# Two transformer blocks in one program: when clears, dense tables, gathers and a branch are placed

## The chip, the cores and the metric

The kernel runs on one core of a Trainium2 chip. The metric is the time of one execution on the device, in microseconds; the number before the change is the median of three runs. One more execution was recorded by the hardware profiler. Its trace gives each instruction's start and duration on the core's engines: PE (TensorE, matrix products and transposes), DVE (VectorE), ACT (ScalarE), POOL (GpSimd) and SP (SyncE, which here only issues DMAs). ACT and POOL issue DMAs too, each in its own instruction stream, in order.

## The reference

The input x has 512 tokens of 1024 channels, everything in fp32. Cut to what matters here:

```
first block:   h = rms_norm(x);  u = h @ w_in
               x += [rms(conv(u)), rms(attention(u))] @ w_out      # 12 heads of 64
               x += cross_attention(rms(x), rms(mem))              # 256 memory tokens
               x += moe(rms(x), w1, w3, w2)                        # 32 experts, 1024 x 512
               x  = rms_norm(x) * final_norm_g
second block:  z = rms(x) @ w_in_2                                 # q, k, v, f, u_ssm, two gates
               x += (sig(g1) * forgetting_attention @ w_a
                     + sig(g2) * s5(u_ssm) @ w_s) @ w_out_2
               x += moe(rms(x), w_gate, w_up, w_down)              # 32 experts, 1024 x 256
moe:           per token: best of 4 groups, then 2 of its 8 experts;
               y[token] += gate * (silu(x w1) * (x w3)) w2
```

## The kernel before, in words

**Stages.** `dense1` computes the first block up to its experts, `m1.run` the experts, `dense2` the second block up to its experts, `m2.run` those; at the end SP stores X in four DMAs. The residual X stays on chip as 4 tiles of 128 tokens x 1024. A planner that simulates a timeline orders each engine's instructions from the order of the program; `tc.issue_after(i)` adds, to what is traced in the block on the engine of instruction `i`, an order behind `i`. It gives no order to instructions of another engine.

**Dense products** are made in three passes (L114 to L116) of a high and a low part of the operands (`mm3`). Weights come in units of 1 MB by SP into a ring of two buffers (L141); ACT casts the high part (`wh`, L125), DVE or POOL subtracts the low part (`wl`, L128).

**Start.** `dense1` loads x, two weight units and the memory tokens, transposes x (L227), casts it to columns (ACT L202, DVE L203), sums its squares (ACT L236), and computes masks and rotary tables on DVE. Then come six rounds, each with two heads (`attend`): scores, a maximum on DVE (L541), an exponential on ACT (L542) for each of four row blocks, transposes, a copy by ACT (L550), the product with v; weight units of later rounds are traced between.

**Experts** (`Moe`). The 32 experts go in 16 pairs; a pair's 128 rows are 64 slots of either expert. Before the experts the rows of X and, behind them, the routing weights are written to DRAM (`rows`, 1024 + 33 numbers a token). For a pair, `slots` computes on DVE for each slot its token (or none), `fetch` gathers the rows by an indirect DMA on POOL's queue (L1161), `columns` transposes them, `up` and `down` are the matmuls (L1083, L1105). A slot with no token gathers row 0. The result of a pair is either written to a table `y` in DRAM (`made` in the trace) by an indirect DMA with a bound that drops empty slots (`store`, L1136), or added to X by one-hot matmuls (`scatter`, L1120 to L1123); pairs 14 and 15 are scattered. `y` is cleared beforehand by 16 DMAs of 512 KB on ACT's queue (`clear`, L805). Near the end SP reads `y` back (`load_made`, L1064), in its list of weight loads ahead of the last 4 (first block) or 2 (second block) loads, and DVE adds it to X (`add_made`, L1070). `rest` is a branch with a loop for tokens beyond an expert's 64 slots; the second block computes one such unit always (at pair 9) and enters the loop only for more. Then the last pair is finished (`finish`).

**Second block's start.** Three tables for the state space part are computed during the first experts and written to DRAM: WT and Qs (2 MB each, read back by `ssm.fetch` on ACT's queue, L1403) and M (2 MB, read in 8 DMAs on POOL's queue by `load_M`, L1713). They live in `big_r`, a pool of two 2 MB buffers that the experts' weights use before. WT feeds `states` (L1653), M and Qs feed `outputs` (L1690, L1691). Meanwhile X is transposed and cast (L1758, L202), `norms` computes two norms by a chain of tiny DVE operations (`rsq`, L212 to L219), and X is scaled by ACT (L1846) and POOL (L1847).

**Names in the trace.** `k.last` is the last scatter cast on ACT (L1115). `marks` and `exps` hold the score matmuls and the exponentials. `wfh` (L1747) is a small cast on POOL at the second block's start.

Of the kernel before, what the change touches and what calls it, by code (L numbers as in the profile page):

```python
# [10 lines left out]
F32 = mybir.dt.float32  # L11
# [11 lines left out]
S = 512  # L23
NB = 4
# [343 lines left out]
def dense1(k, a, Xt, m1, m2, ring1, more, dram, dbg):  # L368
# [15 lines left out]
    with ExitStack() as st:  # L384
# [72 lines left out]
        with ExitStack() as s0:  # L457
# [61 lines left out]

            marks = []  # L520

# [5 lines left out]
            def attend(g, h, om, mid=iter(())):  # L527
# [5 lines left out]
                for b in range(NB):  # L533
# [7 lines left out]
                    V.tensor_tensor_reduce(ml, p, lnm[:, lo:lo + 512], -0.125, 3.0e38, op0=OP.add, op1=OP.min, accum_out=nm)  # L541
                    nc.scalar.activation(ml, ml, AF.Exp, bias=nm, scale=-1.0, accum_out=den[:, b:b + 1])  # L542
                    pt = tpt()
# [72 lines left out]
            for g in range(6):  # L616
                om = wk.tile([128, NB, 128], F32, name="om", bufs=1)
                attend(g, 0, om)
                if m1 and g < 4:
                    with tc.issue_after(marks[-4]):  # L620
                        for m in (m1, m2):
                            for i in range(2):
                                m.clear(zero, 2 * g + i)
# [140 lines left out]
class Moe:  # L764
# [9 lines left out]
    spot = after_loads = None  # L774
    deep = 3

    def __init__(self, k, X, ff, w_a, w_b, w_down, gname, gain, wg, bg, wr, br, spare, rows, y):
# [256 lines left out]
    def ahead(self, wt, n, order=()):  # L1034

        self.wt, self.left = wt, n
        self.early = [self.places(2) for _ in range(16)]
        loads = [x for p, W in enumerate(self.early) for x in self.loads((2 * p, 2 * p + 1), W, wt, first=p == 0)]

        i = len(loads) - self.ff // 128  # L1040
        self.made = []
        loads[i:i] = [partial(self.load_made, b) for b in range(NB)]
        order = list(order)
        self.todo = [loads[i] for i in order] + loads[len(order):]
# [94 lines left out]
    def slots(self, wk, ps, n):  # L1139
# [8 lines left out]
        V.tensor_tensor(q[:, 2:3], ab[:, 0:1], ab[:, 1:2], op=OP.add)  # L1148
        V.tensor_scalar(q[:, 0:1], q[:, 2:3], -1.0, 0.0, op0=OP.add, op1=OP.max)
        V.tensor_scalar(q[:, 1:2], ab[:, 1:2], 0.0, float(S), op0=OP.is_gt, op1=OP.mult)  # L1150
        V.scalar_tensor_tensor(q[:, 1:2], q[:, 2:3], -1.0, q[:, 1:2], op0=OP.add, op1=OP.add)
        V.tensor_scalar(q[:, 3:4], q[:, 2:3], 0.0, k.i16[:, 8:9], op0=OP.is_equal, op1=OP.mult)
        V.tensor_add(q[:, 1:2], q[:, 1:2], q[:, 3:4])
        ids = wk.tile([128, 2], I32, name="ids", bufs=5)
        V.tensor_copy(ids, q[:, 0:2])
        return ids

    def fetch(self, pool, idx, name="xr", deep=3):

        xr = pool.tile([128, D + 33], F32, name=name, bufs=deep)  # L1160
        self.k.nc.gpsimd.indirect_dma_start(out=xr, out_offset=None, in_=self.rows, in_offset=bass.IndirectOffsetOnAxis(ap=idx, axis=0))  # L1161
        return xr
# [41 lines left out]
    def experts(self, wk, ps, between=None):  # L1204
# [7 lines left out]
        def fetch(n):  # L1212
            ids = self.slots(wk, ps, n)
            got[n] = (ids, self.fetch(wk, ids[:, 0:1], deep=deep) if n else None)

        for p in range(16):
# [22 lines left out]
            if last:  # L1239
                self.finish(wk, ps, *last)  # L1240
            last = (hg, W, parts, gate, got[p][0], self.slots_T(wk, p) if p >= 14 else None)
            if between:
# [5 lines left out]
            if self.spare and p == 9:  # L1248
                unit = self.extra_up(wk, ps, unit, self.wt, nc.sync)
                self.finish(wk, ps, *last)  # L1250
                last = unit
        self.add_made()
        if self.spare:
            self.rest(wk, ps, self.wt, self.wl)
        else:
            spare = self.room()
            self.rest(wk, ps, Slots([spare] * 2), spare)
        self.finish(wk, ps, *last)

# [125 lines left out]
class Ssm:  # L1385
# [12 lines left out]

    def fetch(self, big):

        t = [big.tile([128, KC, S], F32, name="b") for i in range(2)]
        for d, s in zip(t, self.par):
            self.k.nc.scalar.dma_start(d, s.rearrange("u p n -> p u n"))  # L1403
        self.WT, self.Qs = [x.rearrange("p u (t q n) -> p u t q n", t=2, q=2) for x in t]

# [310 lines left out]
def dense2(k, a, X, ssm, m2, early, dbg):  # L1716
# [4 lines left out]
    with ExitStack() as st:  # L1721
# [24 lines left out]
        wfh, wfl = w1.tile([128, KC, 8], F32R, name="wfh"), w1.tile([128, KC, 8], F32R, name="wfl")  # L1746
        G.tensor_copy(wfh, wf)  # L1747
        G.tensor_sub(wfl, wf, f(wfh))
# [71 lines left out]
        u_unit(0, ws)  # L1820
        ssm.fetch(k.big_r)

# [20 lines left out]
        with tc.issue_after(puts[-1].ins):  # L1843
            ssm.tables(w1)
        for b in range(NB):
            nc.scalar.activation(X[:, b], X[:, b], AF.Copy, scale=r1[:, b:b + 1])  # L1846
            G.tensor_tensor(X[:, b], X[:, b], frow, op=OP.mult)  # L1847
        gate_unit(sgs, 3080, 0)
# [20 lines left out]
        ssm.states(w1, sct, 1)  # L1869
        ssm.load_M(k.big_r)  # L1870
        gate_unit(sgs, 3080, 2)
# [3 lines left out]
        ssm.outputs(w1, sct, tpt, 1)  # L1875
        v_unit(1)

        ysT = k.big_r.tile([128, KC, S], F32R, name="b")
# [171 lines left out]
def whole(ctx, tc, a, out):  # L2050
# [8 lines left out]
             rows=dram.tile([S, D + 33], F32, name="xrow1"), y=dram.tile([2 * S + 128, D], F32, name="made1"))  # L2059
    m1.deep = 2  # L2060
    m2 = Moe(k, X, 256, a["w_expert_gate_2"][0], a["w_expert_up_2"][0], a["w_expert_down_2"][0], "norm_ffn_g_2",
             a["norm_ffn_g_2"][0], a["w_router_group_2"][0], a["b_router_group_2"][0], a["w_router_expert_2"][0], a["b_router_expert_2"][0], spare=True,
# [83 lines left out]
```

## Time and profile before

| | |
|---|---|
| median of 3 runs | 1786.28 us (1783.35 to 1787.2) |
| profiled execution, its own time | 1789.1 us |
| its span, first to last instruction | 1787.5 us |
| PE busy | 1578.6 us (88%) |
| DVE busy | 779.1 us (44%) |
| ACT busy | 548.0 us (31%) |
| POOL busy | 383.6 us (21%) |
| moved by DMA | 431.88 MB, 242 GB/s on average |
| mean granted TensorE clock | 0.963 of full |

The busy shares are averages over stages with different limits. By the windows, the stages are: the start to about 60 us; attention and cross attention to about 500 us; the first experts to about 1037 us; the second block's dense part to about 1490 us; its experts to the end. A row of waits says which instruction's end came last before an engine went on; "issue" there means that nothing in the profile explains the wait.

### The profile page before, as it was taken

To read this page: it belongs to the slowest core of one execution; us is meant where nothing else is said; L and a number is where in the kernel's file an instruction comes from. 1 tells how busy PE (TensorE), PEld (TensorE's weight loads), DVE (VectorE), ACT (ScalarE), POOL (GpSimd) and SP (SyncE) were. 2 spreads that over 40 slices of the span, in tenths; PEclk is the share of its full clock that TensorE was granted. 3 is DMA by queue.
4 is the path that set the end of the run, shared out by engine and by line. 5 is a ranking of instruction groups with operands and counts; after the bars stand their busy time and mean duration, and the time that the engine had idled before them with its cause. 6 is when DMAs were issued, how large, how long until landed. Compare 5 with 4: busy or idle time off the path is not lost. (4 is left out here: it accounts for less than half of the span.)

```text
span 1787.5 us, 24321 instructions
## 1 busy us (share of the span) xinstructions
PE 1578.6 (88%) x9257; PEld 1070.1 (60%) x9257; DVE 779.1 (44%) x1984; ACT 548.0 (31%) x1212; POOL 383.6 (21%) x523
## 2 busy tenths in 40 slices
PE   3899999999989998888888777899998998988986
PEld 2799999998983333233232245788997894333332
DVE  2896456655454511121110466714665537311225
ACT  2436656644321211010100042233556422111111
POOL 1131112011122631433240022201212401211110
PEclk8999999999999999999999998899999999998998
DMA  9323123232758999999999964625540846999994
GB/s 297 113 72 107 48 71 119 91 101 82 284 180 340 422 424 425 424 425 425 424 423 427 422 149 53 88 72 95 72 71 25 324 136 221 380 418 418 418 410 166
DMA packets 171080, 431.88 MB, mean 242 GB/s; under 512 B 18526, under 2 KB 105749, under 8 KB 143184
## 3 DMA queue, kind: packets, MB, share of 16 engines
q1 hardware_dynamic: 133616, 378.08, 58.0%
q0 software_dynamic: 11936, 32.21, 5.6%
q10 hardware_dynamic: 25408, 20.00, 3.5%
q8 instruction: 74, 1.21, 0.3%
q14 instruction: 46, 0.38, 0.1%
HBM read 403.38 MB, written 34.74 MB: 245 GB/s over the span
## 5 line engine op out<-in xcount | busy, mean ns | idle before, releaser
L1083 PE MATMUL h<-b,xgr 128*64 128x512 f32 x800 | 222.5, 600 | 23.4 <-DMA b<-in_w_dram 21.5
L115 PE MATMUL mm<-wl,b 128*128 128x256 f32 x832 | 236.5, 285 | 6.9 <-POOL wl L128 4.0
L1083 PE MATMUL h<-w,xgr 128*64 128x512 f32 (+1 forms) x752 | 221.4, 609 | 19.2 <-DMA w<-in_w_dram 14.1
L114 PE MATMUL mm<-wh,b 128*128 128x256 f32 x832 | 236.1, 286 | 2.4 <-DVE sgs L1803 0.9
L116 PE MATMUL mm<-wh,b 128*128 128x256 f32 x832 | 234.6, 284 | 0.0
L128 POOL TENSOR_TENSOR wl<-w,wh 128x1024 fp32r<-128x1024 f32 x38 | 97.1, 2556 | 516.2 <-ACT wh L125 445.2
L125 ACT ACTIVATE wh<-w 128x1024 fp32r<-128x1024 f32 x112 | 118.3, 1058 | 159.4 <-PE mm L115 67.6
L115 PEld LDWEIGHTS mm<-wl,b 128*128 128x128 f32 x832 | 159.0, 191 | 9.0 <-POOL wl L128 4.4
L114 PEld LDWEIGHTS mm<-wh,b 128*128 128x128 f32 x832 | 158.3, 191 | 4.6 <-DVE sgs L1803 1.1
L116 PEld LDWEIGHTS mm<-wh,b 128*128 128x128 f32 x832 | 158.4, 191 | 0.5
L114 PE MATMUL mm<-b,wh 128*128 128x512 f32 x320 | 127.4, 408 | 28.7 <-ACT b L202 15.9
L1105 PE MATMUL o<-b,hgT 128*64 128x512 f32 x448 | 129.9, 641 | 24.7 <-issue 8.9
L1083 PEld LDWEIGHTS h<-b,xgr 128*64 128x64 f32 x800 | 67.0, 137 | 134.1 <-issue 82.6
L1083 PEld LDWEIGHTS h<-w,xgr 128*64 128x64 f32 (+1 forms) x752 | 64.8, 140 | 130.8 <-issue 89.3
L1087 DVE SCALAR_TENSOR_TENSOR hg<-h,gate,hg 128x512 f32<-128x512 f32 (+1 forms) x32 | 19.7, 616 | 261.6 <-PE h L1083 196.6
L115 PE MATMUL mm<-b,wh 128*128 128x512 f32 x320 | 128.6, 403 | 0.0
L116 PE MATMUL mm<-b,wl 128*128 128x512 f32 x320 | 127.0, 402 | 0.2 <-POOL wl L128 0.2
L128 DVE TENSOR_TENSOR wl<-w,wh 128x1024 fp32r<-128x1024 f32 x74 | 94.4, 1276 | 52.8 <-ACT wh L125 52.3
L1105 PE MATMUL o<-w,hgT 128*64 128x512 f32 (+1 forms) x328 | 97.4, 622 | 5.3 <-ACT hgT L1099 2.1
L1105 PEld LDWEIGHTS o<-b,hgT 128*64 128x64 f32 x448 | 40.1, 146 | 87.4 <-issue 74.6
L114 PEld LDWEIGHTS mm<-b,wh 128*128 128x128 f32 x320 | 60.8, 192 | 44.8 <-ACT b L202 17.7
L1086 ACT ACTIVATE hg<-h,gate 128x512 f32<-128x512 f32 (+1 forms) x32 | 18.6, 580 | 220.1 <-PE h L1083 171.4
(673 smaller groups left out, 2791.6 us busy)
## 6 DMA issues: line engine op xcount, KB each, us to landing
b<-in_w_dram SPq DMA_DIRECT2D x106, 1024.0 KB
w<-in_w_dram SPq DMA_DIRECT2D x86, 1024.0 KB
b<-in_w_expert_down_dram SPq DMA_DIRECT2D x20, 1024.0 KB
w<-in_w_expert_gate_dram SPq DMA_DIRECT2D x36, 512.0 KB
w<-in_w_expert_up_dram SPq DMA_DIRECT2D x36, 512.0 KB
w<-in_w_in_dram SPq DMA_DIRECT2D x17, 1024.0 KB
b<-in_w_expert_gate_dram SPq DMA_DIRECT2D x30, 512.0 KB
b<-in_w_expert_up_dram SPq DMA_DIRECT2D x30, 512.0 KB
```

The lines of the kernel that those rows point to most:

```text
L114: nc.tensor.matmul(out, sh, mh, start=start, stop=False, skip_group_check=True)
L115: nc.tensor.matmul(out, sh, ml, start=False, stop=False, skip_group_check=True)
L116: nc.tensor.matmul(out, sl, mh, start=False, stop=stop, skip_group_check=True)
L125: nc.scalar.activation(hi[:, :kc, :n], src, AF.Copy)
L128: e.tensor_sub(lo[:, :kc, :n], src, f(hi[:, :kc, :n]))
L1083: nc.tensor.matmul(h[po], xg[:, c, ss], fw[e][c], start=c == 0, stop=c == KC - 1, skip_group_check=True)
L1086: nc.scalar.activation(hg, a, AF.Silu, scale=r)
L1087: nc.vector.scalar_tensor_tensor(hg, b, r, hg, op0=OP.mult, op1=OP.mult)
L1105: nc.tensor.matmul(o[po], hT[:, j, po], W[2][e][half * nt + j], start=j == 0, stop=j == nt - 1, skip_group_check=True)
```

## The change

Five things are changed:

- the clears are ordered behind the third exponential of the first head of each of the first four rounds (an ACT instruction) and no longer behind a score matmul;
- an empty slot's row number lies beyond the table, and the gather has a bound that drops it; the first two or three gather buffers of a block are set to zero by POOL, later ones keep what an earlier pair left;
- the second block stores pair 14 too and reads `y` back behind all weight loads; the first block keeps its numbers;
- in the second block the last pair is finished before the branch, not behind it;
- in the second block's dense part WT is loaded behind the last scatter cast, M behind `wfh`, Qs behind the second `states`; X is scaled by DVE, behind `v_unit(1)`.

```diff
-            marks = []
+            marks, exps = [], []
...
-                    nc.scalar.activation(ml, ml, AF.Exp, bias=nm, scale=-1.0, accum_out=den[:, b:b + 1])
+                    exps.append(nc.scalar.activation(ml, ml, AF.Exp, bias=nm, scale=-1.0, accum_out=den[:, b:b + 1]).ins)
...
-                    with tc.issue_after(marks[-4]):
+                    with tc.issue_after(exps[-2]):
                         for m in (m1, m2):
                             for i in range(2):
                                 m.clear(zero, 2 * g + i)
...
+    stored = 15
+    behind = 0
...
-        i = len(loads) - self.ff // 128
+        i = len(loads) - self.behind
...
-        V.tensor_scalar(q[:, 0:1], q[:, 2:3], -1.0, 0.0, op0=OP.add, op1=OP.max)
...
+        V.scalar_tensor_tensor(q[:, 0:1], q[:, 2:3], -1.0, q[:, 3:4], op0=OP.add, op1=OP.add)
...
-    def fetch(self, pool, idx, name="xr", deep=3):
+    def fetch(self, pool, idx, name="xr", deep=3, clear=False):
         xr = pool.tile([128, D + 33], F32, name=name, bufs=deep)
-        self.k.nc.gpsimd.indirect_dma_start(out=xr, out_offset=None, in_=self.rows, in_offset=bass.IndirectOffsetOnAxis(ap=idx, axis=0))
+        if clear:
+            self.k.nc.gpsimd.memset(xr, 0.0)
+        self.k.nc.gpsimd.indirect_dma_start(out=xr, out_offset=None, in_=self.rows, in_offset=bass.IndirectOffsetOnAxis(ap=idx, axis=0),
+                                            bounds_check=S - 1, oob_is_err=False)
...
-            got[n] = (ids, self.fetch(wk, ids[:, 0:1], deep=deep) if n else None)
+            got[n] = (ids, self.fetch(wk, ids[:, 0:1], deep=deep, clear=n <= deep) if n else None)
...
-            last = (hg, W, parts, gate, got[p][0], self.slots_T(wk, p) if p >= 14 else None)
+            last = (hg, W, parts, gate, got[p][0], self.slots_T(wk, p) if p >= self.stored else None)
...
+        while self.todo:
+            self.todo.pop(0)()
         self.add_made()
         if self.spare:
+            self.finish(wk, ps, *last)
             self.rest(wk, ps, self.wt, self.wl)
         else:
             spare = self.room()
             self.rest(wk, ps, Slots([spare] * 2), spare)
-        self.finish(wk, ps, *last)
+            self.finish(wk, ps, *last)
...
-        ssm.fetch(k.big_r)
+        with tc.issue_after(k.last.ins):
+            ssm.WT = ssm.fetch(k.big_r, 0)
+        with tc.issue_after(wfc.ins):
+            ssm.load_M(k.big_r)
...
-        for b in range(NB):
-            nc.scalar.activation(X[:, b], X[:, b], AF.Copy, scale=r1[:, b:b + 1])
-            G.tensor_tensor(X[:, b], X[:, b], frow, op=OP.mult)
...
-        ssm.load_M(k.big_r)
+        ssm.Qs = ssm.fetch(k.big_r, 1)
...
         v_unit(1)
+        for b in range(NB):
+            V.scalar_tensor_tensor(X[:, b], X[:, b], r1[:, b:b + 1], frow, op0=OP.mult, op1=OP.mult)
...
+    m1.stored, m1.behind = 14, 4
```

## Rows read from the trace of the kernel before

**Rows 1.** Windows: stretch, length, PE PEld DVE ACT POOL busy, PEclk, DMA share, GB/s
```profile
17.00:52.00 35.00, 16.25 (x57) 11.94 (x58) 11.78 (x44) 12.13 (x20) 0.94 (x1) 0.71 0.99 290
...
600.00:980.00 380.00, 326.24 (x1394) 121.95 (x1394) 59.65 (x173) 43.31 (x94) 130.59 (x213) 1.00 1.01 425
1540.00:1735.00 195.00, 172.41 (x696) 65.79 (x695) 40.67 (x126) 31.50 (x85) 29.42 (x53) 0.95 1.02 418
```

**Rows 2.** Windows, in the attention stage
```profile
100.00:200.00 100.00, 99.17 (x821) 97.33 (x821) 75.15 (x136) 55.14 (x132) 23.69 (x13) 0.98 0.26 80
```

**Rows 3.** Tile views (made, xrow, zero): count, ns min/median/max, first and last start
```profile
L1136 POOL DMA_INDIRECT made<-og,ids x28: 983/1036/1511, 580.0 to 1742.0; - x28
L805 ACTq DMA_DIRECT2D made<-zero x16: 607/1670/4019, 17.3 to 44.5; - x16
...
DMA to landing us min/median/max: 5.8/8.4/9.0
...
L824 ACTq DMA_DIRECT2D xrow<-X x8: 367/372/416, 473.5 to 1471.1; - x8
...
L453 POOL MEMSET zero<- x1: 222/222/222, 5.4 to 5.4; 128x128 f32 x1
```

**Rows 4.** Waits of ACT, 17 to 52 us: total us, times, longest
```profile
ACT b L202 <- issue: 13.8, 4, 5.4
ACT wh L125 <- DMA vrows<-in_mix_norm_g_dram: 9.2, 1, 9.2
ACT sq L236 <- issue: 7.3, 2, 5.0
```

**Rows 5.** Windows, at the first experts' end and after
```profile
1011.00:1037.00 26.00, 15.40 (x50) 5.43 (x46) 10.76 (x10) 1.28 (x2) 0.00 (x0) 0.80 0.98 395
1043.00:1052.00 9.00, 4.53 (x24) 2.77 (x22) 8.36 (x16) 4.75 (x11) 3.44 (x5) 0.90 1.00 120
1148.00:1164.00 16.00, 5.21 (x42) 4.81 (x40) 7.31 (x11) 2.32 (x3) 2.38 (x1) 0.75 1.04 110
```

**Rows 6.** Order of time on PE: start, us, instruction, count, idle before it
```profile
1024.20 6.68 PE L1105 MATMUL o<-b,hgT 128*64 128x512 f32 x13 [7.72 <-DMA b<-in_w_dram]
...
1033.74 3.65 PE L1105 MATMUL o<-w,hgT 128*64 128x512 f32 x12 [1.29 <-DMA w<-in_w_dram]
...
1742.71 3.65 PE L1105 MATMUL o<-w,hgT 128*64 128x512 f32 x16
...
1770.23 5.45 PE L1105 MATMUL o<-b,hgT 128*64 128x512 f32 x16 [8.87 <-issue]
```

**Rows 7.** Order of time on DVE
```profile
1018.44 4.93 DVE L1070 TENSOR_TENSOR X<-X,b 128x1024 f32<-128x1024 f32 x4
...
1070.41 2.35 DVE L217 TENSOR_TENSOR rq_u<-rq_i 128x4 f32<-128x4 f32 x1
...
1079.64 0.15 DVE L217 TENSOR_TENSOR rq_u<-rq_i 128x4 f32<-128x4 f32 x1
...
1782.41 0.69 DVE L1123 TENSOR_TENSOR X<-X,y 128x512 f32<-128x512 f32 x1 [0.17 <-PE y L1121]
```

**Rows 8.** Source views of L1847 and L1713, and who waited for L1713
```profile
L1847 POOL TENSOR_TENSOR X<-X,ssrow x4: 2343/2352/2425, 1068.0 to 1075.0; 128x1024 f32<-128x1024 f32 x4
...
L1713 POOL DMA_DIRECT2D b<-scr x8: 628/636/722, 1142.3 to 1146.8; - x8
...
  PE sc L1690: 10.6, 1
```

**Rows 9.** Waits: 1040 to 1085 us; DVE, 1150 to 1180; SP's queue
```profile
PE tp L1782 <- DVE r L1779: 11.7, 1, 11.7
...
DVE s L1699 <- PE sc L1691: 19.8, 1, 19.8
...
SPq L141 <- DVE wl L128: 478.7, 41, 36.8
```

**Rows 10.** Order of time on SP's queue, the output
```profile
1778.58 4.92 SPq L2119 DMA_DIRECT2D out_dram<-X  x4
```

More of the change, by code (lines that the diff above doesn't have):

```diff
@@ L1397, in keep, with fetch @@
         self.r8, self.ur, self.ui = [c.tile([128, 16], F32, name=n) for n in ("ssr8", "ssur", "ssui")]
[L1399 to L1404, printed above, removed]
+    def fetch(self, big, i):
+        t = big.tile([128, KC, S], F32, name="b")
+        self.k.nc.scalar.dma_start(t, self.par[i].rearrange("u p n -> p u n"))
+        return t.rearrange("p u (t q n) -> p u t q n", t=2, q=2)
     def load(self, w):
@@ L1746, in dense2 @@
         wfh, wfl = w1.tile([128, KC, 8], F32R, name="wfh"), w1.tile([128, KC, 8], F32R, name="wfl")
-        G.tensor_copy(wfh, wf)
+        wfc = G.tensor_copy(wfh, wf)
         G.tensor_sub(wfl, wf, f(wfh))
```

## The prediction

> **What bounds the kernel now.** I read the windows first. Between 600 and 980 us (first block's experts) and 1540 and 1735 us (second block's) the DMA engines are full, 425 and 418 GB/s at a share of 1.01 and 1.02, while PE is busy 86% and 88%: these stretches end when their bytes have come [rows 1]. From 100 to 500 us it is PE (99% in the window shown) with ACT 55% busy [rows 2]. Between these lie four places where neither is full, and the change touches all of them: the first 52 us, where PE is busy 16.3 of 35 us although the DMA moves 290 GB/s [rows 1]; the end of the first experts at 1011 to 1037; the start of the second block up to 1164; the last 30 us. So after the windows I read the waits, then the order of time on single engines.
>
> All terms are made against the profiled execution: span 1787.5, its own time 1789.1 us, 2.8 above the median of 1786.28.
>
> **1. The clears.** Sixteen DMAs of 512 KB on ACT's queue. Their old tie, to a matmul, held nothing: they issue from 17.3 to 44.5 us, each holding ACT's sequencer 0.61 to 4.0 us (median 1.67) [rows 3]. In 17 to 52 us ACT idles 13.8 us before the column casts L202 and 7.3 before the squares L236 for nothing but "issue" [rows 4]; PE and DVE wait for these casts. Tied to an exponential, an ACT instruction on ACT's own queue, they must leave this place. The start gets back 13.8 + 7.3 = 21.1 us. Bounds: 29 to 30 if the 9.2 us wait of the first cast of weights [rows 4] goes too, since a clear stands just before it; 12 if the late half of x and the DVE's own 12 us of work [rows 1] end later than ACT. I take 21.
>
> They come back in four groups of four, in heads 0, 2, 4 and 6. A lone 512 KB store from ACT takes 0.37 us to issue, a clear 0.61 at best [rows 3], so a group holds ACT 2.4 us, or 4 x 1.67 = 6.7 if the queue backs up: 10 to 27 us in all. Behind the clears on ACT stand the next exponential, the copies of transposed scores and the casts of the next weight unit, and PE waits for those; but ACT is idle 45% of that window [rows 2], and between the two heads PE has a whole weight unit in hand. I take 3 lost, bounds 0 and 27.
>
> **2. Empty slots not gathered.** 1024 token choices fall on 16 x 128 = 2048 slots, so at least half of each gather's 128 rows of 4,228 bytes are fetched for nothing: 64 x 4,228 x 15 = 4.1 MB a block. The first block is limited by bytes from its start to the reads of `made`: 4.1 MB / 425 GB/s = 9.6 us. The second: 9.7; but PE's own work is 172 of 195 us there [rows 1], so I count 8 (bounds 5 and 9.7). The store to `made` already carries a bound of the same kind and its POOL instruction takes 1.04 us, which is what a bound may cost POOL at most per gather, on an engine that is busy 131 of 380 us here [rows 1, 3]: nothing on the path. Five memsets are added, 128x1057 each; the 128x128 one took 0.22 us [rows 3], so at most 1.8 each. They need only a free buffer and stand before gathers that wait for DVE; 0, or 9 us if none is covered.
>
> **3. The tables' loads leave the end of the first experts.** From 1011 to 1037 the DMA moves 395 x 26 = 10.3 MB [rows 5], of which 4.2 are the two tables on ACT's queue; PE stands 7.7 us for the last expert's down weights and starts at 1024.2 [rows 6]. Without the tables 6.1 MB remain, 14 to 15 us: the weights are there by 1026. Next in line is the branch, which PE passes only after DVE's eight additions of `made`; their last four end at 1023.4 [rows 7]. So PE starts at most 1 us sooner, but no longer runs out: 32 matmuls took to 1037.4, 13.2 us; 16 take 3.65 at the full clock [rows 6], hence 7.3 to 10. Gain 4 (2 to 6).
>
> **4. Start of the second block.** X's scaling leaves ACT and POOL. While POOL's four products (2.35 us each, 1068 to 1077 [rows 8]) run, DVE's tiny operations of the norm's chain take 2.3 us instead of 0.15 [rows 7], and PE waits 11.7 us for that chain [rows 9]. About five such operations shrink: 10 to 11 us. Against it: M's load, 2.1 MB in small pieces, now runs from 1041 beside the first weights. The weights alone move at 120 GB/s with the engines full, M at 110, also full [rows 5], so M's 19 us and WT's 2.1 MB (5 us at the expert rate) fall in the stretch in which PE waits for its first unit. Before the change that unit's matmuls start at 1053, about 12 us after M would start. Every us of delay up to 11.7 eats the gain, each beyond it costs. I take 10 of delay: net 1, bounds -8 (delay 19) and +10.
>
> The Trainium skill, "DMA: Bandwidth & Descriptors", section "Queues, rings and completion order", says that each DMA engine takes turns, packet by packet, among the queues that have work. The two rows on full engines don't show what two queues do together; by equal turns the first weights would come as late as M, and this term would be the -8 of the bounds.
>
> M early, though, removes the one wait it caused: PE stood 10.6 us for it [rows 8]. The Qs table takes its place as the late one: it waits for WT's buffer, free after the states' matmuls near 1142, on ACT's queue (behind it stand the gate's sigmoid and weight casts); 2.1 MB in one DMA need 5 us at the expert rate, PE wants it at 1154. Gain 9; 2 if it moves at M's rate. X's four new operations, some 1.23 us each like DVE's 128x1024 additions [rows 7], come where DVE idles 19.8 us [rows 9]: 0, or 5.
>
> **5. The second block's end.** Pair 14 is stored, not scattered; all weights precede the reads of `made`; the last pair is finished ahead of the branch. Removed: PE's 8.9 us before the last down matmuls [rows 6], which is the branch waiting for DVE's additions. Next bound: DVE. It has 8 x 1.23 (`made`) + 8 x 0.69 (scatter) + 1.5 (casts) = 16.9 us to do [rows 7]; the first read of `made` now waits for that store (issue near 1748, 8.4 to land [rows 3]), so it starts near 1760 and ends near 1777 against 1783.1: 6 gained. Added: the output's four stores, which overlapped the last additions, all come after the branch; four issues take 4.9 us [rows 10], the last needs about 3 more, 8 against 4.4; branch 0 to 2. Net +2, bounds -5 and +7.
>
> **Sum.** 21 - 3 + 9.6 + 8 + 4 + 1 + 9 + 2 = 51.6, so 1789.1 - 51.6 = 1737.5; taken from the median, 1735.
>
> **Rivals.**
> - *ACT's issue time lands on PE after all.* For: PE is at 99%, it has no slack to give. Against: ACT's idle 45%. The start's 21 us less 27: 1735 + 24 = 1759. Chance 0.15.
> - *The clears don't move*, as the first tie didn't bind: 1735 + 18 = 1753. Against: that tie named PE, this one the clears' own engine. 0.06.
> - *The tables starve the second block:* term 4 at -8 and Qs at M's rate: 1735 + 9 + 7 = 1751. 0.12. This is what the rule of equal turns in the Trainium skill ("DMA: Bandwidth & Descriptors", "Queues, rings and completion order") would do to it.
> - *Slower: each clear waits on the weight loads.* At the start ACT stood 9.2 us until a small SP load had landed [rows 4], with a clear next in line; if a clear must wait for an earlier load of SP, and that load for its buffer (SP waits 478.7 us in 41 times for DVE to release one, 11.7 each [rows 9]), 16 clears hold ACT 187 us, beyond its idle half. It decides from 3.2 us uncovered per clear on (16 x 3.2 = 51.6); with half hidden 1735 + 94 = 1829. Against: the X store of 512 KB on that queue took 0.37 us without such a wait [rows 3]. 0.05.
> - Forecast 0.54, its own range 1718 to 1752; better than that (no delay by M, the 9.2 us also gone) 0.08, near 1712.
>
> The range 1708 to 1762 leaves out 0.05 above 1790, and a part of the outer cases. Under 0.2% (3.6 us) is no change that this kernel's runs can tell; only a mixture of the bad cases gives it: 0.02. Faster 0.93, slower 0.05.
>
> **What would show it.** Right: no clears before 100 us, ACT's "issue" waits gone, the first attention exponential some 21 us earlier (129.7 before); full-engine stretches of the experts about 10 us shorter at the same GB/s; DVE's tiny operations at 0.15 us when the norm's chain runs; no wait of PE for M; PE going straight from the last transposes into the down matmuls, and a gap ahead of the output stores instead. Wrong: PE below 95% between 100 and 300 us; the second block's first weight cast more than 30 us after the last scatter cast (14 before); Qs as a releaser of PE; the experts' stretch equally long with fewer bytes, which would mean that something other than bytes limits it.

## The result and the profile after

The changed kernel takes 1736.54 us (median of 4 runs, 1734.27 to 1743.17) against 1786.51 for the kernel before beside it (4 runs): a ratio of 0.973, 95% interval 0.970 to 0.976. Run again later it took 1736.71 us (5 runs, 1734.30 to 1741.70; ratio 0.972, 0.970 to 0.974). The forecast was 1735. The sum came out; several of its terms did not.

The trace read here is of an execution of 1743.17 us, span 1741.5, mean granted clock 0.958. A second trace, of the repeat (1736.71, span 1735.1, clock 0.966), is used beside it. Piece by piece the two differ by up to 2.6 us (table below), so that much in a single trace means nothing.

Windows of the changed kernel, columns as in [rows 1] (line numbers here and below are those of each run's own kernel, a few off the first):

```profile
17.00:52.00 35.00, 31.75 (x174) 26.26 (x174) 32.99 (x95) 18.82 (x30) 6.87 (x5) 0.95 0.43 132
100.00:200.00 100.00, 97.53 (x794) 95.20 (x792) 56.44 (x118) 57.82 (x141) 15.18 (x8) 0.97 0.44 132
560.00:960.00 400.00, 346.69 (x1500) 131.41 (x1499) 75.54 (x231) 45.83 (x100) 139.41 (x237) 0.98 1.01 425
1500.00:1690.00 190.00, 171.09 (x685) 65.30 (x682) 40.60 (x126) 30.57 (x81) 27.71 (x47) 0.94 1.01 410
```

Between 17 and 52 us PE is now busy 31.75 of 35 us (16.25 in [rows 1]). In the attention stage it loses less than 2 us in 100 to the clears [rows 2]. The first experts still run at 425 GB/s; the second block's no longer quite.

The clears (tile view), the first weight casts (order of time on ACT), and the software queue (packets, MB, share; 32.21 MB before):

```profile
L808 ACTq DMA_DIRECT2D made<-zero x16: 520/964/3152, 105.1 to 219.4; - x16
```

```profile
9.40 2.00 ACT L125 ACTIVATE wh<-w 128x1024 fp32r<-128x1024 f32 x2 [0.17 <-DMA w<-in_w_in_dram]
```

```profile
q0 software_dynamic: 12080, 24.03, 4.6%
```

The clears moved. The weight cast waits 0.17 us, where it waited 9.2 [rows 4]. And that queue moves 8.18 MB less, as the forecast had it.

**Milestones.** Lengths in us between points that every trace shows: the start to the store of the first block's routing weights; the first to the last gate product of its experts (taken where ACT's SiLU on it starts); from there to the last scatter cast on ACT; to `Rb`, the end of the norm's chain; to the second block's routing weights; its first to last gate product; to the span's end. (The 12.8 to 13.2 us from a routing store to the first gate product are left out.) Below the first three rows stand the experiments.

| kernel | start and attention | experts 1 | their end | to Rb | dense 2 | experts 2 | end |
|---|---|---|---|---|---|---|---|
| before | 533.5 | 461.0 | 30.1 | 45.4 | 406.0 | 252.9 | 32.5 |
| changed | 507.4 | 456.3 | 28.3 | 51.9 | 387.6 | 255.6 | 28.4 |
| changed, again | 505.1 | 458.4 | 28.4 | 49.8 | 385.5 | 253.0 | 29.0 |
| clears alone | 507.0 | 462.7 | 35.7 | 53.1 | 400.7 | 254.5 | 32.4 |
| full gathers | 504.3 | 462.7 | 28.7 | 51.5 | 387.5 | 255.8 | 29.0 |
| old start of block 2 | 507.2 | 456.3 | 36.5 | 52.6 | 400.4 | 248.7 | 28.9 |
| old end | 506.9 | 458.3 | 27.2 | 51.9 | 384.8 | 254.6 | 32.6 |
| scaling late | 505.0 | 456.5 | 27.4 | 46.5 | 384.9 | 246.5 | 30.6 |
| casts late | 507.2 | 458.6 | 27.6 | 51.2 | 393.1 | 255.4 | 28.4 |
| branch first | 504.5 | 456.7 | 29.1 | 50.0 | 384.8 | 250.8 | 28.9 |
| these three | 505.3 | 457.4 | 28.6 | 45.9 | 395.4 | 250.9 | 28.9 |
| scaling and branch | 504.0 | 457.9 | 28.3 | 46.7 | 384.9 | 245.5 | 28.6 |
| clears and casts | 505.6 | 464.2 | 33.5 | 45.8 | 403.4 | 256.9 | 31.7 |
| all three, M held | 502.1 | 458.0 | 26.9 | 36.6 | 391.5 | 256.2 | 28.4 |

Two pieces of the changed kernel became longer or did not shrink: the way to Rb, and the second block's experts. Order of time on ACT, then DVE, then PE, at the second block's start:

```profile
1004.96 0.69 ACT L1118 ACTIVATE og<-o,gate 128x512 fp32r<-128x512 f32 x1 [2.74 <-PE o L1108]
1005.27 0.37 ACTq L1411 DMA_DIRECT2D b<-sWT  x1
1020.06 2.00 ACT L125 ACTIVATE wh<-w 128x1024 fp32r<-128x1024 f32 x2 [14.41 <-DMA w<-in_w_in_dram]
1021.97 0.61 ACT L1777 ACTIVATE nsq<-X 128x512 f32<-128x512 f32 x1
...
1023.20 1.24 ACT L202 ACTIVATE b<-tp,gm 128x512 fp32r<-128x512 f32 x2
...
1044.11 0.16 DVE L1784 TENSOR_TENSOR r1t<-r 128x4 f32<-128x4 f32 x1
1044.18 6.95 DVE L1886 SCALAR_TENSOR_TENSOR X<-X,r,ssrow 128x1024 f32<-128x1024 f32 x4
...
1051.19 0.15 DVE L1785 TENSOR_TENSOR r1t<-r1t,s 128x4 f32<-128x4 f32 x1
...
1023.91 1.22 PE L114 MATMUL mm<-b,wh 128*128 128x512 f32 x2 [11.48 <-ACT b L202]
...
1055.73 1.08 PE L1790 MATMUL tp<-ident,r 128*128 128x128 f32 x4 [3.38 <-DVE r L1787]
```

Both are matters of order on one engine. ACT's first instruction after the scatter is now a weight cast that waits 14.4 us for its DMA, and squares and column casts, which need nothing of that DMA, stand behind it; PE idles 11.5 us. On DVE the four scalings of X, which nobody needs for a long time, stand between two tiny operations of the norm's chain. Neither order is written in the change: the planner chose both. The tiny operations themselves take 0.15 us again (2.35 in [rows 7]), and PE's wait for M [rows 8] is gone.

### The profile page after: what moved, and what is told of

It reads as the page before. It is cut to its first block, busy times and chain, and to the rows that moved or that the text cites. A ratio compares the mean times of both kernels' runs of the same rounds, so it can differ in the third digit from the quotient of the medians.

```text
span 1741.5 us, 24303 instructions
## 1 busy us (share of the span) xinstructions
PE 1575.2 (90%) x9241; PEld 1073.1 (62%) x9241; DVE 769.0 (44%) x1977; ACT 542.6 (31%) x1207; POOL 381.8 (22%) x525
## 3 DMA queue, kind: packets, MB, share of 16 engines
q0 software_dynamic: 12080, 24.03, 4.6%
## 5 line engine op out<-in xcount | busy, mean ns | idle before, releaser
L114 PE MATMUL mm<-wh,b 128*128 128x256 f32 x832 | 235.7, 286 | 1.4 <-ACT b L202 0.8
L116 PE MATMUL mm<-wh,b 128*128 128x256 f32 x832 | 234.5, 284 | 0.0
L114 PEld LDWEIGHTS mm<-wh,b 128*128 128x128 f32 x832 | 158.2, 191 | 3.4 <-ACT b L202 1.0
L116 PEld LDWEIGHTS mm<-wh,b 128*128 128x128 f32 x832 | 158.3, 191 | 0.6
L1108 PE MATMUL o<-b,hgT 128*64 128x512 f32 x448 | 135.6, 652 | 18.0 <-DVEq L1335 9.3
L114 PE MATMUL mm<-b,wh 128*128 128x512 f32 x320 | 127.0, 409 | 13.3 <-ACT b L202 11.5
L116 PE MATMUL mm<-b,wl 128*128 128x512 f32 x320 | 127.2, 401 | 3.0 <-POOL wl L128 2.7
L114 PEld LDWEIGHTS mm<-b,wh 128*128 128x128 f32 x320 | 61.3, 193 | 28.9 <-ACT b L202 12.2
```

Of the source, the lines that this page charges most:

```text
L114: nc.tensor.matmul(out, sh, mh, start=start, stop=False, skip_group_check=True)
L116: nc.tensor.matmul(out, sl, mh, start=False, stop=stop, skip_group_check=True)
L1108: nc.tensor.matmul(o[po], hT[:, j, po], W[2][e][half * nt + j], start=j == 0, stop=j == nt - 1, skip_group_check=True)
```

## The experiments

Ratios are to the kernel before, timed beside each, with 95% intervals. Theory A is the prediction's own sum; theory B was read from the two traces.

**1. The clears alone**, on the kernel before.

```diff
...
-                    with tc.issue_after(marks[-4]):
+                    with tc.issue_after(exps[-2]):
```

> The kernel before, with the clears tied to the third exponential of the head and nothing else changed. Theory A (the prediction's own sum: 21 us back at the start, 3 lost in the attention): 18 us faster than before, 1768 us. Theory B (read from the two traces: the first score maximum comes 29.6 us earlier, the last one 25.9): 26 us faster, 1760 us, with the first score maximum near 99 us. Rival (ACT's issue time lands on PE): 0 to 8 us faster, 1778 us or more, PE below 95% between 100 and 300 us.

1773.58 us (6 runs), ratio 0.9926 (0.9905 to 0.9947), 15 us faster: less than either theory. Theory B was right on the mechanism: the first score maximum came at 98.6 us and the first routing store 26.5 us early. But 11 us net were given back in code that was not touched: 1.7 in the experts, 5.6 at their end, 7.7 before Rb, 1.6 in the second experts, against 5.3 won in between. Ahead of Rb this kernel, too, has the order on ACT shown above; experiment 11 tests whether that makes the 7.7. Waits of PE, 1030 to 1175 us, total, times, longest:

```profile
PE mm L114 <- ACT b L202: 10.5, 1, 10.5
PE tp L1782 <- DVE r L1779: 9.8, 1, 9.8
PE sc L1690 <- issue: 9.0, 1, 9.0
```

The third, named "issue", is the wait for M: the last of M's eight loads landed at 1146.9 us and PE went on at 1147.2.

**2. Full gathers**, on the changed kernel.

```diff
-        V.scalar_tensor_tensor(q[:, 0:1], q[:, 2:3], -1.0, q[:, 3:4], op0=OP.add, op1=OP.add)
+        V.tensor_scalar(q[:, 0:1], q[:, 2:3], -1.0, 0.0, op0=OP.add, op1=OP.max)
...
-            got[n] = (ids, self.fetch(wk, ids[:, 0:1], deep=deep, clear=n <= deep) if n else None)
+            got[n] = (ids, self.fetch(wk, ids[:, 0:1], deep=deep, clear=False) if n else None)
```

> The changed kernel, but an empty slot again gathers row 0 and the five memsets are gone; nothing else differs, and what is computed is the same. Theory A (the prediction: bytes limit both blocks' experts, 8.2 MB at 425 GB/s): 17.6 us slower than the changed kernel, about 1754 us. Theory B (read from the traces: the first block's experts became 4.7 us shorter up to the last pair's gate product, the second block's 0.3 us between the first and the fifteenth pair's, because PE's own order of work ends last there): 4 to 6 us slower, about 1742 us. Rival (the memsets and the bound cost what the bytes give): within 2 us of the changed kernel.

1742.27 us, ratio 0.9752 (0.9734 to 0.9771), against 0.9718 (0.9698 to 0.9738) of the repeat: about 6 us, theory B, though the two intervals just touch. In the traces the first experts have it (462.7 against 456.3 and 458.4). The second block's take 255.8 with full gathers and 255.6 or 253.0 without: 4.1 MB fewer there bought nothing that two traces can tell.

**3. The old start of the second block**, on the changed kernel.

```diff
-        with tc.issue_after(k.last.ins):
-            ssm.WT = ssm.fetch(k.big_r, 0)
-        with tc.issue_after(wfc.ins):
-            ssm.load_M(k.big_r)
+        ssm.WT, ssm.Qs = ssm.fetch(k.big_r, 0), ssm.fetch(k.big_r, 1)
...
-        ssm.Qs = ssm.fetch(k.big_r, 1)
+        ssm.load_M(k.big_r)
...
-            V.scalar_tensor_tensor(X[:, b], X[:, b], r1[:, b:b + 1], frow, op0=OP.mult, op1=OP.mult)
...
+            nc.scalar.activation(X[:, b], X[:, b], AF.Copy, scale=r1[:, b:b + 1])
+            G.tensor_tensor(X[:, b], X[:, b], frow, op=OP.mult)
```

> The changed kernel with the second block's start as it was: WT and Qs loaded together on ACT's queue during the end of the first experts, M behind the second states, X scaled by ACT and POOL. Theory A (the prediction: 4 at the first experts' end, 1 in the norm's chain, 9 for the wait on M): 14 us slower than the changed kernel, 1750 us, with a wait of PE for M near 10 us again. Theory B (traces: 1.8 us at the first experts' end, 12.9 between the last scatter cast and the first outputs matmul): 14.7 us slower. Rival (the early loads starve the second block's first weights, so undoing them costs little): 0 to 4 us slower.

1757.87 us, ratio 0.9828 (0.9808 to 0.9847), 21 us slower than the changed kernel: more than A or B, and the rival is out. Waits of PE, 1013 to 1150 us:

```profile
PE mm L114 <- ACT b L202: 10.4, 1, 10.4
PE tp L1790 <- DVE r L1787: 9.5, 1, 9.5
PE sc L1698 <- issue: 8.8, 1, 8.8
```

The waits for the norm, beside POOL's products, and for M are back (the third: M's last load landed at 1140.8 us, PE went on at 1141.2). The experts' end is 8.1 us longer with the tables' loads in it (36.5 against 28.4). The second experts, 4 us shorter, hide a part.

**4. The old end**, on the changed kernel.

```diff
-    stored = 15
-    behind = 0
+    stored = 14
+    behind = 2
...
         if self.spare:
-            self.finish(wk, ps, *last)
             self.rest(wk, ps, self.wt, self.wl)
         else:
             spare = self.room()
             self.rest(wk, ps, Slots([spare] * 2), spare)
-            self.finish(wk, ps, *last)
+        self.finish(wk, ps, *last)
```

> The changed kernel with the second block's end as it was: pair 14 scattered, the table read back ahead of the last two weight loads, the branch ahead of the last pair's end. Theory A (the prediction: 6 us gained by DVE starting on the sums earlier and PE not waiting for the branch, 4 lost because the output's stores come after the branch): 2 us slower than the changed kernel, 1738.5 us. Theory B (traces: from the last pair's gate product to the end 32.5 us before and 28.4 after, but that product itself comes 2.7 us later in its stage): 1.4 us slower. Rival (the late reads and the late output stores cost more than the branch did): 1 to 4 us faster than the changed kernel.

1737.06 us, ratio 0.9719 (0.9692 to 0.9745): no difference from the changed kernel. PE's wait of 8.9 us at the branch is back and the end is 3.6 us longer than in the repeat, but the last gate product comes 14.4 us behind the one before it, where the changed kernel needs 17.3.

**5 to 8. Three edits to the orders found, alone and together**, on the changed kernel: X's scaling tied behind the third gate unit's last product on DVE (about 60 us later); the first weight casts tied behind the sixth column cast on ACT; in the first block the branch ahead of DVE's eight sums of `made`.

```diff
...
-        for b in range(NB):
-            V.scalar_tensor_tensor(X[:, b], X[:, b], r1[:, b:b + 1], frow, op0=OP.mult, op1=OP.mult)
+        with tc.issue_after(gated.ins):
+            for b in range(NB):
+                V.scalar_tensor_tensor(X[:, b], X[:, b], r1[:, b:b + 1], frow, op0=OP.mult, op1=OP.mult)
...
-        with tc.issue_after(k.last.ins):
+        with tc.issue_after(cast.ins):
             ws = k.split_unit(spool, k.load_unit([w_in[:, 1544:1800]]), G)
...
-        self.add_made()
         if self.spare:
+            self.add_made()
             self.finish(wk, ps, *last)
             self.rest(wk, ps, self.wt, self.wl)
         else:
             spare = self.room()
             self.rest(wk, ps, Slots([spare] * 2), spare)
+            self.add_made()
             self.finish(wk, ps, *last)
```

> The changed kernel with X's scaling on DVE tied behind the gate unit's last product, 60 us later; in the changed kernel its four operations (6.95 us) stand inside the norm's chain of tiny DVE operations, and PE waits 3.4 us for that chain's end. Theory B (order on DVE is the cost): PE's wait for the norm goes, 3 to 7 us faster than the changed kernel, 1730 to 1733 us. Rival (the chain is covered by PE's slow matmuls at half clock and by POOL's weight part, so nothing is won): within 2 us.

1723.54 us, ratio 0.9644 (0.9623 to 0.9666): 13 us faster than the changed kernel. Rb comes 3.3 us sooner than in the repeat and PE waits 0.5 us for the norm, as expected of the scaling; 6.5 more come from the second experts, and those nobody had foreseen.

> The changed kernel with ACT's casts of the second block's first weight unit tied behind the sixth column cast. In the changed kernel, and in the one with the clears alone, these casts stand at the head of ACT's order and wait 14 us for their weights, with the squares and column casts behind them, and PE idles 11.5 us; in the kernel before they stood behind four column casts. Theory B (this order, which the planner chose anew, takes back 7 to 8 us of what the clears gave): 6 to 8 us faster than the changed kernel, 1729 to 1731 us, the norm's Rb 45 us after the last scatter cast in place of 52. Rival (PE waits for the weights in any order, since their casts come no earlier): within 2 us.

1749.31 us, ratio 0.9780 (0.9754 to 0.9805): 12 us slower; theory B failed. The column casts did come 7 to 10 us earlier. But POOL, no longer held by the weights' low parts, issued M at 1014.9 us, 13 earlier than the changed kernel did. Waits of this kernel, 1020 to 1056 us:

```profile
ACT wh L125 <- DMA w<-in_w_in_dram: 23.7, 1, 23.7
...
PE mm L114 <- ACT wh L125: 14.6, 1, 14.6
```

That is the prediction's rival of starved weights. The change itself had just missed it: M moved there while SP's queue had almost nothing to move (1036 to 1048 us: 1.39 MB of M, 0.02 MB of weights). It is not the whole of the 12 us, since PE's 11 us wait for the column casts is gone in return: from the last scatter cast to the second block's first score maximum this trace needs 6.1 us more than the repeat (228.7 against 222.6), and the rest is spread over other pieces.

> The changed kernel with the first block's branch ahead of DVE's eight sums of the table (they stood ahead of it, and PE waited 9.3 us at the branch). Theory A (the branch is what holds PE at the first experts' end): 5 to 9 us faster than the changed kernel. Theory B (the last down weights land near 996 us, 2 us behind the branch, so bytes end next): 2 to 5 us faster, with PE's wait for DVE replaced by one for the weights. Rival (no change, DVE's sums still end last): within 1 us.

1732.42 us, ratio 0.9688 (0.9666 to 0.9709), 4 us faster than the repeat, with intervals that overlap. The experts' end did not become shorter (29.1 us against 28.3 and 28.4). Order of time on PE, in the changed kernel and in this one:

```profile
994.45 5.28 PE L1108 MATMUL o<-b,hgT 128*64 128x512 f32 x10 [9.29 <-DVEq L1335]
```

```profile
992.05 5.88 PE L1108 MATMUL o<-b,hgT 128*64 128x512 f32 x10 [9.47 <-DVE X L1073]
```

With the branch out of the way the wait is the same length and carries another name. These matmuls read nothing that the sums write, but they also wait for the last 1 MB of weights, whose load is issued behind the reads of `made` (at 974.6 and 972.2 us). The semaphore of that load has its last update at 994.22 us in the changed kernel and at 991.91 in this one, 0.2 and 0.1 us before PE starts; the branch in the one and the last sum in the other end within 0.15 us of it. So the bytes end here too, as theory B had it, but with nothing between them and the branch. Beside the repeat no piece is more than 2.2 us shorter (the second experts), which two traces of one kernel differ by as well: where the 4 us lie is not shown.

> The three edits before this one together: scaling late, weight casts behind column casts, the first block's branch ahead of the sums. Theory B: the two at the second block's start share one stretch, so 9 to 12 us for them and 2 to 5 for the branch, 11 to 16 us faster than the changed kernel, near 1723 us. Rival: part is given back in the second block's experts, which begin earlier with fewer weights on the chip: 6 us faster, 1731 us.

1738.21 us, ratio 0.9719 (0.9696 to 0.9742): the two gains are gone again, because M goes first here too (issued at 1012.8; experiment 12 tests this).

**9 to 12. The repeat, the best pair, and two tests of the explanations.**

> The changed kernel as it is, once more, so that the variants have it beside them on one chip. Expected: 1736.5 us, a ratio to the kernel before of 0.972 to 0.973.

1736.71 us, as expected.

> The changed kernel with X's scaling tied late and the first block's branch ahead of the sums. Theory B: the scaling's 13 us stand, and the branch adds nothing of its own, because the last down weights land at the same moment as DVE's sums end; its 4 us came from a new order of work further on: 1722 to 1725 us. Rival (the two add up): 1719 us.

1724.07 us (1721.18 to 1727.09), ratio 0.9646 (0.9628 to 0.9663): theory B, the two do not add up.

Experiment 11 is the kernel of experiment 1 with the second edit of 5 to 8:

> The kernel before with the clears alone, and ACT's casts of the second block's first weight unit tied behind the sixth column cast. Moving the clears alone won 27 us up to the first gather and 15 at the end; the table of milestones puts 8 of the 12 that were given back between the last scatter cast and the norm's Rb (45.4 us before, 53.1 with the clears alone), where the weight casts had come to stand first. Here M still loads late, so it cannot get in the weights' way, as it did when the same tie was put into the changed kernel. Theory B (that order took the 8 us): Rb 45 to 47 us behind the last scatter cast, 6 to 8 us faster than the clears alone, 1766 us. Rival (the order costs nothing, PE then waits for the weights): within 2 us of the clears alone, Rb 51 us or more behind.

1769.66 us (6 runs), ratio 0.9890 (0.9869 to 0.9912): 4 us faster than the clears alone, with intervals that just overlap. Rb is 45.8 us behind the scatter cast (53.1), so the order on ACT did take those 7 us up to Rb. More than half of it went again: from the scatter cast to the first product of `outputs` 3.0 us are left (129.0 to 126.0). PE now reached `outputs` sooner and waited longer there for M, 12.2 us in place of 9.0:

```profile
PE sc L1690 <- DMA b<-scr: 12.2, 1, 12.2
```

Experiment 12 is all three edits, with M tied behind the first unit's second low part on POOL:

```diff
-        with tc.issue_after(wfc.ins):
+        with tc.issue_after(low.ins):
             ssm.load_M(k.big_r)
```

> The changed kernel with X's scaling late, the branch ahead of the sums, the weight casts behind the sixth column cast, and M's load tied behind POOL's second weight part of the first unit, where the changed kernel happened to have it. With the weight casts late and M free, M issued 13 us earlier and the second weight unit landed so late that ACT waited 24 us and PE 15 for it. Theory B (M ahead of the second weight unit is what made that variant slower): no such wait, PE's 11 us for the column casts gone too, 1715 to 1722 us. Rival (weights are late with M in either place): a wait of PE of 10 us or more for the second unit's cast, 1733 us or more.

1729.12 us, ratio 0.9675 (0.9659 to 0.9690). It differs from the three edits together only in M's place, 10 us later, and is 9 us faster; Rb stands at 36.6 us against 45.9. DMA of the casts-late kernel, 1028 to 1044 us, while the second weight unit is on its way with M (q0) and WT (q10) beside it; q1 is SP's queue (packets, MB, share of the engines):

```profile
DMA packets 1226, 2.61 MB, mean 163 GB/s; under 512 B 81, under 2 KB 491, under 8 KB 1225
...
q0 software_dynamic: 409, 1.34, 56.8%
q10 hardware_dynamic: 406, 0.83, 31.0%
q1 hardware_dynamic: 410, 0.42, 18.3%
```

And of this kernel, 1014 to 1020 us, the same unit with WT alone beside it:

```profile
DMA packets 1475, 2.27 MB, mean 379 GB/s; under 512 B 14, under 2 KB 723, under 8 KB 1474
...
q10 hardware_dynamic: 755, 1.54, 68.5%
q1 hardware_dynamic: 719, 0.73, 34.7%
```

The engines are full in both (shares of 1.07 and 1.04). With M in flight they move 163 GB/s, without it 379, and the weights 26 against some 120. The three queues move the same number of packets, 406 to 410: the weights, with 1 KB in a packet, get a third of the turns and a sixth of the bytes, and M's turns, with some 3 KB in a packet, take more than half of the time. The total was still short of theory B: dense 2 and the second experts are 6.6 and 10.7 us longer than with scaling and branch.

**Where the second experts' time goes.** Their first four gate products span 42 to 47 us in nine of the fourteen traces (the kernel before and both of the changed one among them) and 37 to 38 in five: old start, scaling late, branch first, these three, and scaling with branch. In all five POOL issues the block's first store to `made` 11 to 12 us after the first gate product, in the nine 17 to 23 us after it. What the late store does, in the changed kernel (order of time on POOL, DVE, PE):

```profile
1474.16 0.31 POOL L1237 COPY gate<-xr 64x1 f32<-64x1 f32 x1 [5.85 <-DMA xr<-xrow,ids]
...
1475.36 1.51 POOL L1139 DMA_INDIRECT made<-og,ids  x1 [0.64 <-DVE y L1148]
...
1484.76 1.20 POOL L1166 DMA_INDIRECT oxr<-xrow,idx  x1 [0.54 <-DVE q L1153]
...
1483.69 0.17 DVE L1158 CAST ids<-q 128x2 int32<-128x2 f32 x1 [6.98 <-DMA made<-og,ids]
...
1493.89 0.19 DVE L1323 CUSTOM_DVE_ANT_0 ot<-oxr,oe 128x32 f32<-128x32 f32 x1 [8.04 <-DMA oxr<-xrow,idx]
...
1494.61 0.70 PE L1099 MATMUL pt<-ident,hg 128*128 128x128 f32 x2 [4.44 <-DVE hg L1090]
```

The store stands behind a gate copy that waits for a gather. DVE's next list of slots waits 7.0 us until the store has landed; only then POOL gathers the extra unit's rows; DVE waits 8.0 us for those with the pair's gate product behind, and PE for that. With scaling late the store is issued at 1458.32 us, ahead of that copy, and PE does not wait for DVE there. PE's 4.4 us are what this chain shows; that the late store costs all of the 7 us by which the first four products differ is argued from the order in fourteen traces, since no run moves the store alone. Over the whole stage the five are 2 to 8 us shorter than the repeat.

## Why the prediction was right, and where it was not

The sum was 51.6 us; the traces gave 46.0 (changed) and 52.4 (again). Tested one at a time, the clears (1), the gathers (2), the second block's start (3) and its end (4) are worth 15, 6, 21 and 0 us, 42 of the 50; they need not add, each edit being planned anew. By the sum's steps:

1. **Clears at the start, +21: too small.** The first score maximum moved from 129.0 to 99.4 us, 29.6: the wait of the first weight cast [rows 4], which I had left to the upper bound (29 to 30), went as well. A wait whose named cause was a DMA fell with the clear ahead of it on ACT.
2. **Clears in the attention, -3: right.** The last maximum gained 25.9 (336.9 to 311.0), so 3.7 were lost; ACT's issues took 0.96 us in the median.
3. **Gathers in the first block, +9.6: about 6** (experiment 2). The bytes went as worked out; but the stage's last stretch is PE's (960 to 983.5 us: busy 23.4 of 23.5), where bytes buy nothing.
4. **Gathers in the second block, +8: nothing to measure.** I set PE's 172 of 195 us [rows 1] against full DMA engines and called it bytes. This stretch's own list of waits, in the kernel before, says otherwise: 3.3 us of PE's 23.3 end on a DMA, most on DVE and ACT (lines below). With full gathers PE is busy 171.1 of 190 us there (1505 to 1695), without 171.1 (1500 to 1690). The prediction's own sign of being wrong, a stretch equally long with fewer bytes, came true here. Waits of PE in the kernel before, 1540 to 1735 us, the five longest:

```profile
PE pt L1096 <- DVE hg L1087: 6.9, 6, 1.2
PE o L1105 <- ACT og L1134: 5.5, 5, 1.1
PE h L1083 <- ACT xgr L1176: 3.3, 7, 0.5
PE h L1083 <- DMA w<-in_w_expert_up_dram: 2.7, 1, 2.7
PE o L1105 <- ACT hgT L1099: 1.5, 3, 0.5
```
5. **Tables off the first experts' end, +4: 1.7 in the traces.** Put back into the changed kernel they cost 8.1 (experiment 3), because with the clears moved that end had grown from 30.1 to 35.7 (experiment 1). There PE's wait for the last down weights is 15.9 us in place of 7.7: WT's load is issued at 982.8 us, ahead of the last load of those weights (985.5), where in the kernel before it came behind it (1011.5 and 1009.1). That WT took turns with the weights and so made them late is argued from this order, not tested.
6. **The norm's chain at the second block's start, +1 (bounds -8 to +10): -4.4 to -6.5 up to Rb**, inside the bounds but by another mechanism. I priced M's transfer against the first weights. They were not delayed: they came 14.7 to 15.1 us after the scatter cast (14.2 before); what came in its place was the order on ACT (7 us up to Rb, experiment 11) and X's scaling inside the chain (3 to 5, experiment 5). I had put the scaling "where DVE idles" because it is traced there; an operation without an order behind it goes where the planner likes.
7. **M's wait gone, +9: 18.4 to 20.5 in dense 2.** Part of this is the other side of term 6, because PE's products changed places around Rb: 72 of the weight products (L114 to L116) stand between the scatter cast and Rb in place of 60, and 24 narrow ones between Rb and `outputs` in place of 50. Terms 6 and 7 are better measured together: from the last scatter cast to the second block's first score maximum it is 236.9 us before, 225.2 and 222.6 after, 11.7 to 14.3 gained where the two had 10. The 10.6 us went in full and PE never waited for Qs (2.6 us in the casts-late kernel alone). Part of the rest is PE's clock: from Rb to `outputs`, in steps of 20 us, it was granted 0.88, 1.00, 0.91 and 0.80 of full before, the first behind the 11.7 us wait for the norm and the last with the wait for M in it, and 0.91, 1.00 and 1.00 after. The share of the clock is not separated.
8. **The end, +2: 3.5 to 4.1 from the last gate product on**, given back by that product's later place; net 0 (experiment 4). Order of time on PE, DVE and SP's queue, to set beside [rows 6, 7, 10]:

```profile
1716.26 5.07 PE L1108 MATMUL o<-b,hgT 128*64 128x512 f32 x16 [0.47 <-ACT hgT L1102]
...
1732.32 0.69 DVE L1126 TENSOR_TENSOR X<-X,y 128x512 f32<-128x512 f32 x1 [0.46 <-PE y L1124]
...
1733.34 2.89 SPq L2130 DMA_DIRECT2D out_dram<-X  x4
```

PE's 8.9 us wait became 0.5, and the gap ahead of the output's stores came as forecast: the last sum ends at 1733.0 us and the span 8.5 later (4.4 before).

So the total was near partly by luck: terms 1, 8, and 6 with 7, were short by 12 to 15 us, terms 3 to 5 long by about 14. One sum of the rivals is off: no delay by M and the 9.2 us gone, 9 each, make 1717, not 1712. Of the rivals, ACT's issue time landing on PE and clears that don't move are refuted: PE is 97.5% busy beside them, and the first is issued at 105 us. So are clears that wait on the weight loads: none holds ACT for more than 3.2 us. The starved second block did not happen in the change, and did, at 14.6 us, as soon as M went 13 us earlier. The rule of the Trainium skill ("DMA: Bandwidth & Descriptors", "Queues, rings and completion order"), that each DMA engine takes turns, packet by packet, among the queues with work, agrees with that trace: 409, 406 and 410 packets of the three queues in the same 16 us.

The best version measured is the changed kernel with X's scaling tied late: 1723.54 us, 0.9644 of the kernel before; with the branch ahead of the sums as well it is the same within the noise (0.9646). It does not have the 10 us that experiment 12 won before Rb, of which 6.6 went again by the second routing store; joining the two in an order that keeps the early store was not tried.

## What to carry to other kernels

Where a planner orders the engines, an edit reorders code far behind it: after each one, look at what each engine does first in every later stage, and tie down what waits for a DMA (a cast of weights) behind what is ready, and what nobody needs soon (X's scaling) behind the urgent chain. Price bytes saved only in the stretch where the waits end on DMA, and check a stage's own wait list before calling it limited by bytes. When a wait loses its named cause and keeps its length, look for a second one that ended at the same moment.

## What the runs showed of the hardware

- The gather with a bound leaves out the dropped rows' bytes: its queue moves 24.03 MB in place of 32.21, and the rows of half the slots of 30 gathers are 8.12 MB. It takes POOL as long: 1.04 us an issue against 1.01.
- A 512 KB DMA issued from ACT held it for 0.52 to 3.15 us in the attention (median 0.96), beside 132 GB/s, against 0.61 to 4.02 at the start (1.67) [rows 3], beside 290.
- Three queues with work moved equal numbers of packets (409, 406 and 410), not of bytes. With M's load among them the full engines moved 163 GB/s, without it 379.
- The second block's first weight unit comes slowly with nothing beside it: 0.68 MB in 8 us, 85 GB/s, at 96% of the engines' time (casts late, 1008 to 1016 us). Its successor, in the same 1 KB pieces, does not: 0.84 MB in 4 us at 82% (the kernel before, 1050 to 1054). The 120 GB/s of [rows 5], which the prediction took for what such weights move at, has both in its window. Why the first is slow is open.
